# Attention row maxima in one reduce over two PSUM banks, carried to the score row by DMA

## The chip, the cores and the metric

The kernel runs on one core of one Trainium2 chip. The metric is the device time of one execution in microseconds (us). TensorE (PE) multiplies matrices, VectorE (DVE), ScalarE (ACT) and GpSimd (POOL) work on vectors, and every DMA is issued by SyncE (SP), which does nothing else. Each engine takes its instructions in program order, and an instruction that waits holds up everything behind it on its engine.

## The reference, cut to what matters

A two-layer trunk acts on 512 latent tokens of width 1024 with 256 context tokens in front. Each layer has a convolution branch, eight heads of latent attention (MLA) and eight heads of grouped-query attention (GQA), gates that merge the three, an output projection, and a channel mixer (FFN). The attention part, per head:

```python
def attention_block(q, k, v, scale):
    s = jnp.einsum('bqhgd,bkhd->bhgqk', q, k).astype(jnp.float32) * scale
    p = jax.nn.softmax(s, axis=-1)
    return jnp.einsum('bhgqk,bkhd->bqhgd', p.astype(v.dtype), v)
```

Latent queries see all 768 keys. In layer 0 the context queries are computed as well and see the 256 context keys; in layer 1, the last, they are not needed.

## The kernel before

All matrices are split into a high and a low part, and each product is three matmuls. The order of the work is written out by hand: the program is a list of stages, and the order of the code is the order on each engine. Stages of a layer are: norm, convolution branch, latents and token projections, 24 steps of gate projection, `kvproj` (keys and values), attention (`Attention.run`), merge, output projection and FFN. In layer 0, gate steps and FFN steps also call `bg_step`, which streams two 512 KB blocks of modulation weights (`w_mod`) and multiplies them for later use; `mod` holds one PSUM bank open while such a group is under way.

Attention runs 16 heads, 8 GQA then 8 MLA, each in units: in layer 1 six units (six tiles of 128 keys against the 512 latent queries), in layer 0 a seventh one for the context queries. A unit `i` of head `h` does the following, on PE in this order:

- `score(h, i)`: the transposed scores `st` of 128 keys, two passes for GQA, three for MLA. The last pass has one more row of contraction: a row of ones in the keys against a row of the negated row maxima in the queries (`mrow`: row 64 of `q2` in GQA, row 96 of `qh` in MLA). So the maximum is subtracted inside the matmul. ACT then takes exp twice (`pe`, and rounded `ph`), and POOL or DVE the difference `pl`.
- `pv`: three matmuls `ox` of the unit that stands `LAG` = 4 units back. After the last key tile of a head, which therefore falls in unit 3 of the next head (layer 1) or unit 2 (layer 0, whose context part follows in unit 3), DVE copies the sum to `u`. `norm1` then starts the division by the row sums: `sd<-u` writes one row to DRAM, `rc<-sd` reads it back over 128 partitions. Later `norm2` takes the reciprocal, writes it (`sd<-rc`) and broadcasts it (`rb<-sd`). The last two heads of layer 1's order and of layer 0's (`fast`) do it with matmuls, `nt` and `nb`.
- `max_rows(i)` of the **next** head, for `i` below 4: scores of 128 queries against all 768 keys in two matmuls, into two PSUM tiles of one bank (512 and 256 wide), and a maximum by DVE over each. After the fourth, `mcat` takes the larger of each pair into a column set of `mxs`. In layer 0 `max_rows(4)` and `(5)` do the same for the context queries of the head itself.
- transposes for the head after next (`trans_a`, `trans_b`).

In the head's last unit, ahead of the next head's first score, `fin(True)` transposes `mxs` on PE into PSUM (`mt`), and ACT copies four pieces of 1x128, times -1, to the score row. `fin(False)` does two pieces for the context queries in unit 3. For the first head, `kvproj` runs all four `max_rows` one after the other at its third step, and `fin(True)` at its sixth.

PSUM is one pool of 8 tiles of one bank each. In heads 13 to 15 the attention also reloads 16 tiles `rel` from DRAM for the merge (384 KB each in layer 0, 256 KB in layer 1).

Of the kernel before, what the change touches and what calls it, by code (L numbers as in the profile page):

```python
# [47 lines left out]
class Feeder:  # L48
    """Streams weight blocks: DRAM -> raw -> (hi, lo) split, ahead of their use."""

# [45 lines left out]
def trunk_kernel(ctx: ExitStack, tc: tile.TileContext, x_t, ctx_t, cc, vec, grow, ident, rope,  # L96
# [14 lines left out]
    smp = ctx.enter_context(tc.tile_pool(name="smp", bufs=12))  # L111
    psp = ctx.enter_context(tc.tile_pool(name="psp", bufs=8, space=bass.MemoryType.PSUM))
    drp = ctx.enter_context(tc.tile_pool(name="drp", bufs=1, space=bass.MemoryType.DRAM))
    ctx.enter_context(tc.manual_schedule())

    def big(s, dt=F32):
# [8 lines left out]
    def psum(s):  # L125
        return psp.tile([128, 512], F32, tag="ps", name=nm(s))

# [11 lines left out]
    def cpV(o, i):  # L139
        V.tensor_copy(out=o, in_=i)  # L140
# [20 lines left out]
    am = [[const.tile([128, KD, 2], F32, name=f"am{l}{i}") for i in range(2)] for l in range(L)]  # L161
    mxs = [const.tile([128, 128], F32, name=f"mxs{i}") for i in range(2)]
    kr = const.tile([128, 6, ROPE], F32, name="kr")
# [6 lines left out]
    ones_d = dram("ones", [1, T])  # L170
    s_d = [[dram("sd", [2, T]) for _ in range(16)] for _ in range(L)]

    steps = []
# [259 lines left out]
    def setup():  # L433
# [12 lines left out]
        V.memset(cs[:], 0.0)  # L446
        for m in mxs:
            P.memset(m[:], 0.0)
        st["n1"] = Norm(0, 0, st["X"], [XS, CS])
# [12 lines left out]
    def layer(l):  # L462
# [422 lines left out]
        for i in range(24):  # L885
            gate(i)
            if i < 22:
                bg_step()

        def attn_pre(_):  # L890
            st.pop("H"), st.pop("ln")
            gate_spill()
        add([], attn_pre)

# [94 lines left out]
        class Head:  # L989
            def max_rows(self, t):  # L990
                w, k = self.maxq(t)
                if t in (0, 4):
                    self.m2 = small("mx2")
                for i, (c0, n) in enumerate(((0, 512), (512, 256)) if t < 4 else ((512, 256),)):
                    p = psum("mx")
                    mm(p[:, 0:n], lhsT=w, rhs=k[:, c0:c0 + n], start=True, stop=True)  # L996
                    o = 2 * (t % 4) + i
                    V.tensor_reduce(out=self.m2[:, o:o + 1], in_=p[:, 0:n], axis=AX.X, op=ALU.max)  # L998
                if t == 3:
                    self.mcat(True)  # L1000
                if t == 5:
                    self.mcat(False)

            def mcat(self, x):
                mx = mxs[0 if x else 1]
                n = 4 if x else 2
                mv = mx.rearrange("p (a b) -> p a b", b=32)[:, 0:n, 0]
                m3 = self.m2[:, 0:2 * n].rearrange("p (a b) -> p a b", b=2)
                if x:
                    tt(V, mv, m3[:, :, 0], m3[:, :, 1], ALU.max)  # L1010
                else:
                    cpV(mv, m3[:, :, 0])

            def fin(self, x):
                mx = mxs[0 if x else 1]
                p = psum("mt")
                nc.tensor.transpose(p[:, 0:128], mx[:], idn[:])
                for i in range(4 if x else 2):
                    c0 = (0 if x else 512) + i * 128
                    cpA(self.mrow(slice(c0, c0 + 128)), p[32 * i:32 * i + 1, 0:128], -1.0)  # L1020

# [97 lines left out]
        class Attention:  # L1119
# [8 lines left out]
            def prologue(self, i):  # L1128
                hd = self.heads[0]
                if i == 0:  # L1130
                    warm(AF.Exp)
                    hd.trans_a()
                    hd.trans_b()
                elif i == 2:
                    for t in range(4):
                        hd.max_rows(t)
                    self.heads[1].trans_a()
                    self.heads[1].trans_b()
                elif i == 5:
                    hd.fin(True)  # L1140

# [119 lines left out]
            def run(self, _):  # L1261
# [3 lines left out]
                for g in range(len(seq) + LAG):  # L1265
                    h, i = seq[g] if g < len(seq) else (16, g - len(seq))
                    hd = self.heads[h] if h < 16 else None
                    nx = self.heads[h + 1] if h + 1 < 16 else None
                    if nx and i == nu - 1:
                        nx.fin(True)  # L1270
                    if hd:
# [12 lines left out]
                    if hd and not last:  # L1284
                        if i == 0:
                            hd.max_rows(4)
                        if i == 1:
                            hd.max_rows(5)
                        if i == 3:
                            hd.fin(False)  # L1290
                    if hd:
# [33 lines left out]
                st.pop("VT"), st.pop("rl")  # L1325
                self.heads = None
        add([], lambda b: st["A"].run(b))

# [178 lines left out]
        def up(j):  # L1507
# [19 lines left out]
            elif j > 1:  # L1527
# [7 lines left out]
                one(1)  # L1535
                bg_step()

        j0 = done = 0
        for gi, gn in enumerate(GROUPS):
# [24 lines left out]
            j0 += gn  # L1564

    setup()
    bg += [(0, r, kt) for r in (1, 2) for kt in range(KD)]
# [5 lines left out]
    for s in steps:  # L1573
        b = feeder.take(len(s.blocks))
        pump(*s.budget)
        s.fn(b)
        while feeder.n_done < feeder.n_take:
            feeder.release()


# [85 lines left out]
```

## Time and profile before

| | |
|---|---|
| Median of 3 runs | 2548.25 us (2548.14 to 2550.47) |
| Profiled execution, first to last instruction | 2548.6 us (the only time that was recorded of it) |
| TensorE busy | 2395.1 us, 94% |
| VectorE busy | 1612.0 us, 63% |
| ScalarE busy | 1052.0 us, 41% |
| GpSimd busy | 675.9 us, 27% |
| Mean granted TensorE clock | 0.976 |

The profiled execution lies 0.35 us above the median. Layer 0's attention runs from about 535 to 757 us, layer 1's from about 1874 to 2058 us. Busy shares are means over the whole; what an instruction is worth has to be read in the stage where it stands.

### The profile page before, as it was taken

What the parts mean: (1) busy time and instruction counts of PE and PEld (TensorE: products, weight loads), DVE (VectorE), ACT (ScalarE), POOL (GpSimd) and SP (SyncE); (2) the same over time, 40 slices, a digit from 0 to 9 for tenths busy, and PEclk for the clock granted to TensorE, in tenths of its full rate; (3) what the DMA queues carried; (4) which work ended last, traced back from release to release, by engine and by line L of the source; (5) the groups of instructions that cost most, each with busy time, mean ns of one, the idle gap of its engine ahead of it and who ended that gap; (6) DMA issues with size and microseconds to landing.
All of it is one profiled execution on the core that took longest, in us unless ns stands there. A gap on an engine that the chain in (4) does not pass through costs nothing.

```text
span 2548.6 us, 33199 instructions
## 1 busy us (share of the span) xinstructions
PE 2395.1 (94%) x12538; PEld 1954.5 (77%) x12538; DVE 1612.0 (63%) x2669; ACT 1052.0 (41%) x1832; POOL 675.9 (27%) x505
## 2 busy tenths in 40 slices
PE   7977999988999999999999999888989999999999
PEld 4876777766778878888888887776766778888887
DVE  6889773389864465434344458889579865655454
ACT  3453422477751234323232234444376732434332
POOL 1575400136543221000000003433036541201000
PEclk9988999999999999999999999999999999999999
DMA  6111366611144412323322222233421154232332
GB/s 253 56 54 54 118 217 199 230 44 51 42 141 134 162 50 83 103 89 107 99 100 91 92 94 89 66 91 94 148 89 45 29 178 162 75 108 86 101 103 75
DMA packets 109197, 267.71 MB, mean 105 GB/s; under 512 B 20022, under 2 KB 28860, under 8 KB 109036
## 3 DMA queue, kind: packets, MB, share of 16 engines
q1 hardware_dynamic: 109036, 265.58, 31.8%
q8 instruction: 99, 1.62, 0.3%
q14 instruction: 62, 0.51, 0.1%
HBM read 231.31 MB, written 31.60 MB: 103 GB/s over the span
## 4 chain that ended last, share of the span: by engine, by line
PE 59%; DVE 22%; issue 10%; ACT 5%; DMA 2%; POOL 1%; SPq 0%; ACTq 0%; POOLq 0%; DVEq 0%
PE up L223 22%; PE pz L223 16%; PE bx L223 7%; DVE acc L146 6%; DVE lo L143 3%; PE gt L223 2%; DVE mx L998 2%; PE st L1148 2%; PE gl L223 2%; ACT hi L137 1%; PE qp L706 1%; DVE qm L146 1%; DVE rst L143 1%; PE mx L996 1%; PE ox L1177 1%
## 5 line engine op out<-in xcount | busy, mean ns | idle before, releaser
L143 DVE TENSOR_TENSOR lo<-raw,hi 128x1024 fp32r<-128x1024 f32 (+4 forms) x282 | 353.7, 1261 | 475.3 <-ACT hi L137 470.0
L137 ACT ACTIVATE hi<-raw 128x1024 fp32r<-128x1024 f32 (+4 forms) x298 | 283.2, 962 | 422.2 <-PE pz L223 170.9
L223 PE MATMUL up<-hl,hi 128*128 128x512 f32 (+1 forms) x1088 | 333.7, 354 | 6.1 <-DVE hl L146 5.8
L223 PE MATMUL up<-hh,hi 128*128 128x512 f32 (+1 forms) x1088 | 332.6, 353 | 2.0 <-DVE fc L146 2.0
L223 PE MATMUL up<-hh,lo 128*128 128x512 f32 (+1 forms) x1088 | 330.7, 352 | 0.8 <-DVE lo L143 0.8
L143 POOL TENSOR_TENSOR acc<-acc,ct 128x497 f32<-128x497 f32 (+14 forms) x180 | 236.3, 1335 | 283.9 <-ACT ct L137 280.7
L143 POOL TENSOR_TENSOR pl<-pe,ph 128x512 fp32r<-128x512 f32 x176 | 233.8, 1343 | 225.4 <-ACT ph L1157 81.1
L146 DVE SCALAR_TENSOR_TENSOR fc<-up,vct,fc 128x511 f32<-128x511 f32 (+1 forms) x264 | 162.1, 656 | 184.4 <-ACT fc L1485 182.6
L143 POOL TENSOR_TENSOR gl<-fc,gh 128x768 fp32r<-128x768 f32 (+1 forms) x44 | 69.3, 1574 | 784.0 <-ACT gh L137 681.5
L223 PEld LDWEIGHTS up<-hh,hi 128*128 128x128 f32 x1088 | 183.5, 190 | 42.7 <-ACT fc L1485 11.7
L223 PEld LDWEIGHTS up<-hl,hi 128*128 128x128 f32 x1088 | 184.4, 190 | 35.1 <-DVE hl L146 6.6
L223 PEld LDWEIGHTS up<-hh,lo 128*128 128x128 f32 x1088 | 185.3, 191 | 30.7 <-DVE lo L143 1.3
L223 PE MATMUL gt<-hh,lo 128*128 128x512 f32 x576 | 176.2, 360 | 15.5 <-DVE lo L143 15.5
L146 DVE SCALAR_TENSOR_TENSOR acc<-y,vct,acc 128x497 f32<-128x497 f32 (+14 forms) x180 | 185.1, 1074 | 1.6
L223 PE MATMUL gt<-hh,hi 128*128 128x512 f32 x576 | 178.4, 364 | 0.5 <-ACT hi L137 0.5
L223 PE MATMUL gt<-hl,hi 128*128 128x512 f32 x576 | 175.8, 359 | 0.0
L1485 ACT ACTIVATE fc<-up,vct 128x512 f32<-128x512 f32 (+1 forms) x132 | 88.4, 703 | 197.9 <-PE up L223 197.9
L223 PE MATMUL pz<-gl,hi 128*128 128x512 f32 (+1 forms) x528 | 163.5, 358 | 0.0
L223 PE MATMUL pz<-gh,hi 128*128 128x512 f32 (+1 forms) x528 | 163.0, 356 | 0.0
L223 PE MATMUL pz<-gh,lo 128*128 128x512 f32 (+1 forms) x528 | 162.7, 356 | 0.0
L1155 ACT ACTIVATE pe<-st 128x512 f32<-128x512 f32 x208 | 124.4, 599 | 76.5 <-PE st L1148 59.9
L998 DVE TENSOR_REDUCE mx<-mx 128x1 f32<-128x256 f32 (+1 forms) x288 | 139.3, 531 | 20.5 <-PE mx L996 20.2
(300 smaller groups left out, 4846.7 us busy)
## 6 DMA issues: line engine op xcount, KB each, us to landing
raw<-in_w_up_dram SPq DMA_DIRECT2D x88, 512.0 KB
raw<-in_w_mod_dram SPq DMA_DIRECT2D x80, 512.0 KB
raw<-in_w_gate_dram SPq DMA_DIRECT2D x48, 512.0 KB
raw<-in_w_a_dram SPq DMA_DIRECT2D x26, 512.0 KB
gd<-go SPq DMA_DIRECT2D x48, 256.0 KB
gx<-gd SPq DMA_DIRECT2D x48, 256.0 KB
raw<-in_w_dn_dram SPq DMA_DIRECT2D x32, 384.0 KB
raw<-in_w_dn_dram SPq DMA_DIRECT2D x32, 320.0 KB
```

Of the source, the lines that this page charges most:

```text
L137: act(out=o, in_=i, func=AF.Copy, scale=scale)
L143: e.tensor_tensor(out=o, in0=a, in1=b, op=op)
L146: V.scalar_tensor_tensor(out=o, in0=a, scalar=s, in1=b, op0=op0, op1=op1)
L223: mm(p[:, 0:cn], lhsT=w, rhs=a[:, c0:c0 + cn], start=(k == 0 and j == 0), stop=(k == n - 1 and j == 2))
L706: mm(p[i][:, 0:384], lhsT=a, rhs=w[:, i * 384:(i + 1) * 384], start=(k == 0 and q == 0), stop=(k == 2 and q == 2))
L996: mm(p[:, 0:n], lhsT=w, rhs=k[:, c0:c0 + n], start=True, stop=True)
L998: V.tensor_reduce(out=self.m2[:, o:o + 1], in_=p[:, 0:n], axis=AX.X, op=ALU.max)
L1148: mm(p[:], lhsT=a, rhs=b, start=(i == 0), stop=(i == len(ops) - 1))
L1155: act(out=e[:], in_=p[:], func=AF.Exp, scale=hd.scale)
L1177: mm(o[0:65, :], lhsT=vh, rhs=hi[:], start=(t == 0), stop=False)
L1485: act(out=acc[:, c], in_=p[:, 0:s[1]], func=AF.Identity, scale=vcol(o + 1), bias=vcol(V_FB + j + i * KF))
```

## The change

`max_rows` puts its two matmuls into one tile of two banks, and one DVE reduce over 768 columns gives the negated maximum straight into a column of a small tile `mn`. For context queries it is a single bank (`mc`) and a reduce over 256. `mcat`, `fin`, `mxs` and the transposes `mt` are gone. In their place SP issues two DMAs per set of rows: `md<-mn` writes the columns to DRAM in query order, and a second one reads that row into `mrow`. The write goes element by element: neighbours in DRAM come from different partitions.

PSUM is divided anew: 8 single banks outside attention, and from `attn_pre` to the end of `run` 6 single and one double. Since a modulation group would hold a bank through attention, six of the `bg_step` calls move from gate steps of layer 0 to its FFN steps.

```diff
     def psum(s):
-        return psp.tile([128, 512], F32, tag="ps", name=nm(s))
+        return banks["one"].tile([128, 512], F32, tag="ps", name=nm(s))
+
+    def psum2(s):
+        return banks["two"].tile([128, 1024], F32, tag="pd", name=nm(s))
...
             gate(i)
-            if i < 22:
+            if i < 16:
                 bg_step()
...
             gate_spill()
+            psum_layout(6, 1)
...
-                    self.m2 = small("mx2")
-                for i, (c0, n) in enumerate(((0, 512), (512, 256)) if t < 4 else ((512, 256),)):
-                    p = psum("mx")
-                    mm(p[:, 0:n], lhsT=w, rhs=k[:, c0:c0 + n], start=True, stop=True)
-                    o = 2 * (t % 4) + i
-                    V.tensor_reduce(out=self.m2[:, o:o + 1], in_=p[:, 0:n], axis=AX.X, op=ALU.max)
-                if t == 3:
-                    self.mcat(True)
-                if t == 5:
-                    self.mcat(False)
...
+                    self.mn = mnp.tile([128, 8], F32R, tag="mn", name=nm("mn"))
+                if t < 4:
+                    p, n = psum2("mx"), T
+                    for c0, cn in ((0, 512), (512, 256)):
+                        mm(p[:, c0:c0 + cn], lhsT=w, rhs=k[:, c0:c0 + cn], start=True, stop=True)
                 else:
-                    cpV(mv, m3[:, :, 0])
-
-            def fin(self, x):
-                mx = mxs[0 if x else 1]
-                p = psum("mt")
-                nc.tensor.transpose(p[:, 0:128], mx[:], idn[:])
-                for i in range(4 if x else 2):
-                    c0 = (0 if x else 512) + i * 128
-                    cpA(self.mrow(slice(c0, c0 + 128)), p[32 * i:32 * i + 1, 0:128], -1.0)
+                    p, n = psum("mc"), NCTX
+                    mm(p[:, 0:n], lhsT=w, rhs=k[:, NX:T], start=True, stop=True)
+                V.tensor_reduce(out=self.mn[:, t % 4:t % 4 + 1], in_=p[:, 0:n], axis=AX.X, op=ALU.max, negate=True)
+                if t in (3, 5):
+                    t0, nt = (0, 4) if t == 3 else (4, 2)
+                    c = slice(t0 * 128, (t0 + nt) * 128)
+                    md = m_d[l][self.idx][0:1, c]
+                    dma(md.rearrange("o (t p) -> (o p) t", p=128), f(self.mn[:, 0:nt]))
+                    dma(f(self.mrow(c)), md)
...
-                    if nx and i == nu - 1:
-                        nx.fin(True)
...
-                        if i == 3:
-                            hd.fin(False)
...
-                bg_step()
+                bg_step(2 if j in (4, 8, 12, 16) else 1)
```

Three places show how the instructions move. The first is SP in layer 1 in unit 3 of MLA head 1 (`u` and `sd` belong to head 0, whose sum has just been finished; `kh` is a key tile of head 3; `ogd` and what follows stand in the next head). Before:

```order
L1196 DMA sd_213<-u_17783 1x512
L1198 DMA rc_17893<-sd_213 128x4
L1096 DMA kh_17902<-ones_188 1x768
L1243 DMA ogd_186<-oh_17943 128x512
L1244 DMA ogd_187<-ol_17944 128x512
L1203 DMA sd_213<-rc_17893 128x4
L1205 DMA rb_17990<-sd_213 64x512
```

After, where `mn`, `md` and `qh` belong to head 2, whose first score comes three units later (units 4 and 5 of head 1 lie between):

```order
L1196 DMA sd_211<-u_17453 1x512
L1198 DMA rc_17551<-sd_211 128x4
L1021 DMA md_245<-mn_17492 128x4x1
L1022 DMA qh_17458<-md_245 1x512
L1098 DMA kh_17559<-ones_186 1x768
L1243 DMA ogd_184<-oh_17600 128x512
L1244 DMA ogd_185<-ol_17601 128x512
L1203 DMA sd_211<-rc_17551 128x4
L1205 DMA rb_17639<-sd_211 64x512
```

The two new DMAs stand behind both DMAs of `norm1` and ahead of the key row, and the second new one reads what the first wrote.

The second place is PE in layer 1, from the last transpose of unit 4 of MLA head 1 through its unit 5 to the first score of MLA head 2. Before:

```order
L986 MATMUL tp_17935<-idn,qm_14980 96x128
L1017 MATMUL mt_17949<-idn,mxs_96 128x128
L1148 MATMUL st_17955<-ql_17639,kh_17608 128x512
L1148 MATMUL st_17955<-qh_17638,kl_17609 128x512
L1148 MATMUL st_17955<-qh_17638,kh_17608 128x512
L1177 MATMUL ox_17929<-ph_17846,va_16421 65x512
L1178 MATMUL ox_17929<-ph_17846,va_16421 64x512
L1179 MATMUL ox_17929<-pl_17847,va_16421 65x512
L1148 MATMUL st_17968<-ql_17789,kh_17757 128x512
L1148 MATMUL st_17968<-qh_17788,kl_17758 128x512
L1148 MATMUL st_17968<-qh_17788,kh_17757 128x512
```

After, the same stretch:

```order
L1001 MATMUL tp_17592<-idn,qm_14767 96x128
L1148 MATMUL st_17606<-ql_17322,kh_17291 128x512
L1148 MATMUL st_17606<-qh_17321,kl_17292 128x512
L1148 MATMUL st_17606<-qh_17321,kh_17291 128x512
L1177 MATMUL ox_17586<-ph_17508,va_16215 65x512
L1178 MATMUL ox_17586<-ph_17508,va_16215 64x512
L1179 MATMUL ox_17586<-pl_17509,va_16215 65x512
L1148 MATMUL st_17619<-ql_17459,kh_17427 128x512
L1148 MATMUL st_17619<-qh_17458,kl_17428 128x512
L1148 MATMUL st_17619<-qh_17458,kh_17427 128x512
```

The transpose `mt` is gone from ahead of unit 5, and the very last `st` pass, the first that reads the score row of head 2 (row 96 of its `qh`), stands where it stood.

The third place is DVE in layer 0, units 0 and 1 of MLA head 4 (the reduces into `mx_1508`, and those from `mc`, are the head's context rows). Before:

```order
L998 TENSOR_REDUCE mx_1505_6945<-mx_6946 128x1
L998 TENSOR_REDUCE mx_1505_6945<-mx_6949 128x1
L998 TENSOR_REDUCE mx_1508_6952<-mx_6953 128x1
L140 CAST ph_6939<-pe_6938 128x512
L998 TENSOR_REDUCE mx_1505_6945<-mx_6970 128x1
L998 TENSOR_REDUCE mx_1505_6945<-mx_6973 128x1
L998 TENSOR_REDUCE mx_1508_6952<-mx_6976 128x1
L140 COPY mxs_97<-mx_1508_6952 128x2
L140 COPY u_6860<-ox_6861 65x512
```

After:

```order
L1016 TENSOR_REDUCE mn_6729<-mx_6730 128x1
L1016 TENSOR_REDUCE mn_6734<-mc_6735 128x1
L156 CAST ph_6723<-pe_6722 128x512
L1016 TENSOR_REDUCE mn_6729<-mx_6752 128x1
L1016 TENSOR_REDUCE mn_6734<-mc_6756 128x1
L156 COPY u_6650<-ox_6651 65x512
```

Three reduces per unit become two, and the copy to `mxs` is gone from ahead of the copy of `u`; the four-wide `mxs` operation that stood behind the reduces of unit 3 is gone as well.

## Rows read from the trace of the kernel before

**Rows 1.** The page: busy time of each engine; the chain by line.

```profile
PE 2395.1 (94%) x12538; PEld 1954.5 (77%) x12538; DVE 1612.0 (63%) x2669; ACT 1052.0 (41%) x1832; POOL 675.9 (27%) x505
PE up L223 22%; PE pz L223 16%; PE bx L223 7%; DVE acc L146 6%; DVE lo L143 3%; PE gt L223 2%; DVE mx L998 2%; PE st L1148 2%; PE gl L223 2%; ACT hi L137 1%; PE qp L706 1%; DVE qm L146 1%; DVE rst L143 1%; PE mx L996 1%; PE ox L1177 1%
```

**Rows 2.** Windows, busy us (instructions) by engine, PEclk, DMA share, GB/s.

```profile
455.00:500.00 45.00, 44.26 (x263) 35.07 (x262) 18.86 (x21) 20.76 (x31) 7.37 (x4) 1.00 0.76 261
535.00:600.00 65.00, 55.90 (x272) 37.76 (x272) 59.91 (x124) 48.73 (x110) 44.43 (x40) 0.97 0.15 42
643.00:740.00 97.00, 94.29 (x499) 70.30 (x498) 82.48 (x159) 71.75 (x159) 56.05 (x43) 1.00 0.18 58
860.00:1300.00 440.00, 433.02 (x2470) 366.36 (x2470) 202.16 (x302) 129.32 (x181) 40.42 (x24) 0.99 0.27 93
1951.00:2031.00 80.00, 78.06 (x387) 56.69 (x387) 70.89 (x128) 59.20 (x128) 48.40 (x37) 1.00 0.11 28
```

**Rows 3.** Timeline, a handover in layer 1: start, us, line, operation.

```profile
1984.19 0.69 DVE L140 COPY u<-ox 65x512 f32<-65x512 f32 x1 [0.49 <-PE ox L1179]
...
1984.91 0.23 SPq L1196 DMA_DIRECT2D sd<-u  x1
1986.05 0.33 SPq L1198 DMA_DIRECT2D rc<-sd  x1
1986.43 0.27 SPq L1096 DMA_DIRECT2D kh<-ones  x1
...
1987.66 1.11 ACT L137 ACTIVATE qh<-mt 1x128 fp32r<-1x128 f32 x4
...
1988.82 0.49 PE L1148 MATMUL st<-qh,kh 97*128 97x512 f32 x1
```

**Rows 4.** Waits of TensorE, 1875 to 2060: us in total, times, longest.

```profile
PE mt L1017 <- DVE mxs L143: 5.9, 7, 2.3
```

**Rows 5.** Timeline of SyncE, 1970 to 2001.

```profile
1980.66 0.33 SPq L1203 DMA_DIRECT2D sd<-rc  x1
1982.10 0.45 SPq L1205 DMA_DIRECT2D rb<-sd  x1
```

**Rows 6.** Timeline, end of layer 1's attention.

```profile
2044.03 0.24 SPq L1196 DMA_DIRECT2D sd<-u  x1
2047.96 0.33 SPq L1198 DMA_DIRECT2D rc<-sd  x1
...
2049.55 0.18 DVE L1202 RECIPROCAL rc<-rc 128x4 f32<-128x4 f32 x1 [2.01 <-DMA rc<-sd]
...
2044.85 0.42 PE L1148 MATMUL st<-qh,kh 97*128 97x512 f32 x1
```

**Rows 7.** Timeline, start of layer 0's attention.

```profile
514.65 3.79 DVE L998 TENSOR_REDUCE mx<-mx 128x1 f32<-128x512 f32 x8
...
515.77 1.48 PE L986 MATMUL tp<-idn,gt 128*64 128x128 f32 x6
```

**Rows 8.** Groups of `mxs`: ns min/median/max, first, last start, forms.

```profile
L143 DVE TENSOR_TENSOR mxs<-mx x32: 166/194/1122, 518.5 to 2042.5; 128x4 f32<-128x4 f32 x32
L140 DVE COPY mxs<-mx x16: 169/494/1151, 535.5 to 739.8; 128x2 f32<-128x2 f32 x16
```

**Rows 9.** Timeline, layer 0: three heads and the end.

```profile
608.66 0.24 SPq L1196 DMA_DIRECT2D sd<-u  x1
...
611.88 0.50 PE L1148 MATMUL st<-q,kl 65*128 65x512 f32 x1 [0.33 <-ACT q L137]
...
663.32 0.24 SPq L1196 DMA_DIRECT2D sd<-u  x1
...
668.41 0.40 PE L1148 MATMUL st<-qh,kh 97*128 97x512 f32 x1
...
736.67 0.33 SPq L1198 DMA_DIRECT2D rc<-sd  x1
...
736.59 0.40 PE L1148 MATMUL st<-qh,kh 97*128 97x512 f32 x1
```

More of the change, by code (lines that the diff above doesn't have):

```diff
@@ L111, in trunk_kernel, with psum_layout @@
     smp = ctx.enter_context(tc.tile_pool(name="smp", bufs=12))
-    psp = ctx.enter_context(tc.tile_pool(name="psp", bufs=8, space=bass.MemoryType.PSUM))
+    mnp = ctx.enter_context(tc.tile_pool(name="mnp", bufs=4))
     drp = ctx.enter_context(tc.tile_pool(name="drp", bufs=1, space=bass.MemoryType.DRAM))
     ctx.enter_context(tc.manual_schedule())
+    banks = {"open": []}
+    def psum_layout(single, double):
+        for c in reversed(banks["open"]):
+            c.__exit__(None, None, None)
+        uid[0] += 1
+        banks["open"] = []
+        for key, n, w in (("one", single, 1), ("two", double, 2)):
+            if n:
+                c = tc.tile_pool(name=f"ps{key}{uid[0]}", bufs=n, space=bass.MemoryType.PSUM, reuse_waits="tile")
+                banks[key] = c.__enter__()
+                banks["open"].append(c)
     def big(s, dt=F32):
@@ L161, in trunk_kernel @@
     am = [[const.tile([128, KD, 2], F32, name=f"am{l}{i}") for i in range(2)] for l in range(L)]
-    mxs = [const.tile([128, 128], F32, name=f"mxs{i}") for i in range(2)]
     kr = const.tile([128, 6, ROPE], F32, name="kr")
@@ L171, in trunk_kernel @@
     s_d = [[dram("sd", [2, T]) for _ in range(16)] for _ in range(L)]
+    m_d = [[dram("md", [1, T]) for _ in range(16)] for _ in range(L)]
     steps = []
@@ L446, in setup @@
         V.memset(cs[:], 0.0)
-        for m in mxs:
-            P.memset(m[:], 0.0)
         st["n1"] = Norm(0, 0, st["X"], [XS, CS])
@@ L992, in max_rows @@
                 if t in (0, 4):
-                    self.m2 = small("mx2")
-                for i, (c0, n) in enumerate(((0, 512), (512, 256)) if t < 4 else ((512, 256),)):
-                    p = psum("mx")
-                    mm(p[:, 0:n], lhsT=w, rhs=k[:, c0:c0 + n], start=True, stop=True)
-                    o = 2 * (t % 4) + i
-                    V.tensor_reduce(out=self.m2[:, o:o + 1], in_=p[:, 0:n], axis=AX.X, op=ALU.max)
-                if t == 3:
-                    self.mcat(True)
-                if t == 5:
-                    self.mcat(False)
-            def mcat(self, x):
-                mx = mxs[0 if x else 1]
[L1006 to L1010, printed above, removed]
-                else:
-                    cpV(mv, m3[:, :, 0])
-            def fin(self, x):
-                mx = mxs[0 if x else 1]
-                p = psum("mt")
-                nc.tensor.transpose(p[:, 0:128], mx[:], idn[:])
-                for i in range(4 if x else 2):
-                    c0 = (0 if x else 512) + i * 128
-                    cpA(self.mrow(slice(c0, c0 + 128)), p[32 * i:32 * i + 1, 0:128], -1.0)
+                    self.mn = mnp.tile([128, 8], F32R, tag="mn", name=nm("mn"))
[3 more added lines that the diff above has]
+                        mm(p[:, c0:c0 + cn], lhsT=w, rhs=k[:, c0:c0 + cn], start=True, stop=True)
+                else:
+                    p, n = psum("mc"), NCTX
[7 more added lines that the diff above has]
+                    dma(f(self.mrow(c)), md)
         class GHead(Head):
@@ L1138, in prologue @@
                     self.heads[1].trans_b()
-                elif i == 5:
-                    hd.fin(True)
             def score(self, hd, u):
@@ L1326, in run @@
                 self.heads = None
+                psum_layout(8, 0)
         add([], lambda b: st["A"].run(b))
@@ L1564, in layer @@
             j0 += gn
+    psum_layout(8, 0)
     setup()
@@ L1578, in trunk_kernel @@
             feeder.release()
+    for c in reversed(banks["open"]):
+        c.__exit__(None, None, None)
 def _prep(i):
```

## The prediction

> **What bounds the kernel now.** I read the page first: TensorE is busy for 2395 of 2548.6 us, and the chain that ended last is PE for the most part, with FFN and merge matmuls on top; the reduces `mx` hold 2% of it [rows 1]. So the maxima can matter only inside the two attention stages, and there I read the windows [rows 2]. In layer 0 the GQA heads are bound by DVE (59.91 of 65 us busy, PE 55.90). In the MLA heads of both layers PE is the bound: 94.29 of 97 us in layer 0, 78.06 of 80 in layer 1. Little can be won there, and whatever makes PE wait longer shows in full.
>
> Third, I read one handover in the timeline [rows 3], because the row of maxima is a deadline. DVE copies the finished sum `u` at 1984.19; SP issues `sd<-u` at 1984.91, and `rc<-sd`, which has to see it landed, at 1986.05; the next DMA goes out at 1986.43. Meanwhile ACT copies the four pieces of the next row, 1987.66 to 1988.77, and the `st` pass that reads them starts at 1988.82. That pass stands on PE right behind the end of the copies: already before the change the row is just in time. From `sd<-u` to that pass are 3.91 us.
>
> **The change, part by part.** The new row can't come before this chain: `sd<-u` lands (1986.05 less 1984.91, 1.14 us), `rc<-sd` is issued and the next DMA follows (0.38) [rows 3], the write `md<-mn` lands (M), and the read of the row lands (R). SP takes them in this order, and the maxima are ready earlier, so SP's queue decides, not DVE.
>
> M is not in the trace. The nearest row is `sd<-rc`, a write of 128 short pieces: its reader is issued 1.44 us after it [rows 5]. That is the lower bound, as `md<-mn` writes four times as many pieces, of 4 bytes. The upper bound is a one-row write behind reload traffic, 2044.03 to 2047.96, 3.93 us [rows 6]. I take 1.8, close to the lower end, as SP's queue is quiet in most heads. R lies between 1.14 (`sd<-u`, one row the other way [rows 3]) and 1.59 (`rc<-sd` issued at 2047.96, its reader on DVE at 2049.55 [rows 6]); I take 1.35. The chain is 1.14 + 0.38 + 1.8 + 1.35 = 4.67 us from the issue of `sd<-u`, with ends of 4.10 and 7.04.
>
> The Trainium skill speaks against the change here. Its page "DMA: Bandwidth & Descriptors" says under "Rules for kernel authors" that a last dimension that isn't contiguous becomes one descriptor per element, and under "Anatomy of one DMA" that a DMA has about 2.0 us of fixed cost. By that M + R would be an estimated 4.0 us where I take 3.15, and the sum would come out near 2584; the landings shown here, 1.14 to 1.59 us, are all under its 2.0.
>
> *Layer 1, heads.* The handovers of heads 2 to 14 can be read like the one in [rows 3], 13 in number; from `sd<-u` to the pass they add up to 50.56 us, 3.89 each. With 4.67 the pass comes 0.78 later, and as the next `u` hangs on that pass through PE's order, each delay adds to the next: 13 × 0.78 = 10.1 (2.7 with the low end, 41 with the high). What comes back: `mxs` and its 0.2 us in DVE's order [rows 8] and some overlap of reduces, in the four or five GQA heads where `u` is late on DVE: 2 us. The transpose `mt`, for which PE waited 5.9 us in this layer [rows 4], brings nothing, as PE now waits a little further on, at the pass. ACT loses 1.1 us a head, but it isn't the bound. Net **+8**.
>
> *Layer 1, last head.* Here SP issues five reloads ahead of `sd<-u`, and `rc<-sd` follows 3.93 us later, at 2047.96 [rows 6]. `md<-mn` goes out at about 2048.38, the row is there at 2048.38 + 1.8 + 1.35 = 2051.5. Before, the pass ran at 2044.85 [rows 6]. PE stands for the difference, and everything behind it waits for PE: **+6.7** (6.1 to 9.0).
>
> *Start of each attention.* In `kvproj` four `max_rows` stand one behind the other. Before, the eight reduces ran back to back, 3.79 us from 514.65, while PE had left for the next transposes at 515.77 [rows 7]. With one double tile each pair of matmuls has to wait for the reduce before it. Reduces of 0.95 (3.79 / 4) and pairs of about 0.5 (a pass alone takes 0.49 [rows 3]) alternate: 514.65 + 3 × 1.45 = 519.0, so PE leaves 3.2 later. Twice that is 6.4; part is swallowed in layer 0, whose first heads are bound by DVE. **+5** (0 to 6.4). In the heads the units lie further apart than a reduce lasts, and I cost the single double tile at nothing there; the cover is gone when DVE runs a unit behind.
>
> *Layer 0, GQA heads.* Six handovers, 3.85 us on average (one is 608.66 to 611.88, 3.22 [rows 9]), against 4.67: +4.9. But here DVE is the bound and loses work: the four-wide `mxs` and the context copy, whose medians are 0.19 and 0.49 and that take up to 1.1 beside other work [rows 8], and a little in each reduce; about 1.2 us a head, so `u` is ready earlier by as much: −7. Net **−2** (−6 to +12).
>
> *Layer 0, MLA heads.* A head has one more unit here, so the gap is longer: 663.32 to 668.41 is 5.09 [rows 9], the seven average 5.23. The chain of 4.67 fits in. PE's 2.71 us of idle time in 97 [rows 2] bound the gain: **−2**.
>
> *Layer 0, last head.* As in layer 1, `rc<-sd` comes late, at 736.67, with the pass at 736.59 [rows 9]. The row is there at 737.1 + 3.15 = 740.2, 3.7 later for PE. Part of it lies beside the wait for the divisions, which are late as well: **+2.5**.
>
> *At nothing.* The six modulation steps move from a stretch where PE is busy 44.26 of 45 us to one of 433.02 of 440, and DMA from 0.76 to 0.27 [rows 2]: PE pays the same in both, and the weights have more room. The cover would be gone if blocks came late in the FFN. Six banks instead of eight: the two that are missing are those that `mx` took from each round, so a bank comes round after as many units as before. The SP rows behind the new ones (`kh`, `sd<-rc`) have units to spare.
>
> Sum: 8 + 6.7 + 5 − 2 − 2 + 2.5 = +18.2, against the profile's own 2548.6 us: 2566.8. The median of the runs is 0.35 lower, so I forecast **2566 us**.
>
> **The rivals.**
> - *Slower DMAs.* If the scattered write takes 2.4 and the row 1.6, the chain is 5.5, 0.83 longer. That is 10.8 in layer 1, 5 in layer 0's GQA heads, 1.9 in its MLA heads (5.5 against 5.23), 1.7 in the two last heads: **2585**. For it: 512 pieces of 4 bytes, which no row shows. Against it: no quiet small DMA in the rows takes over 1.6.
> - *A wash.* With the low ends (4.10), layer 1's heads cost 0.7, the last heads 6.1 and 1, the starts 3, and layer 0 gives 7.5 back: +3.3, **2552**. For it: 1.44 and 1.14 are measured landings.
> - *Faster.* The place is the handover, and the deciding point is a chain under 3.9 us, the mean gap of layer 1. Then the pass no longer waits for the row, PE keeps the 5.9 us that it spent at `mt` [rows 4], and layer 0 keeps its relief: 3.3 − 5.9 − 4 for starts that stay hidden = −6.6, **2542**. For it: PE, DVE and ACT all have less to do. Against it: four landings in a row would need 3.9 us, and the smallest that the rows show make 4.10.
>
> **How the numbers follow.** The forecast has 0.48 (2554 to 2577), slower DMAs 0.20, the wash 0.17, faster 0.15. A difference under 0.2% (5.1 us) can't be told from none for this kernel. So slower 0.68, same 0.17, faster 0.15. The range reaches into the rivals at both ends, 2541 to 2590, and leaves out about 0.1 on either side.
>
> **What would show it.** Right: in layer 1 PE's waits at `st` name the DMA of the row, about 1 us a head, and some 6 to 7 us in the last head; `md<-mn` to the row's issue is 1.5 to 2.3 us; PE waits for the `mx` reduce at the start of each attention; DVE's window in layer 0 (535 to 600) gets less busy, and the FFN stays as long as it is. Wrong: no wait for the row at all, a write that takes 3 us or more, PE waiting for the double tile in every head, or a time that moves in the FFN or gate stage rather than in attention.

## The result: 18% slower, 2549 to 3002 us

The changed kernel takes 3001.98 us (median of 4 runs, 2999.83 to 3002.52), the kernel before 2549.34 us beside it: a ratio of 1.1768, with a 95% interval of 1.1751 to 1.1785. The forecast was 2566, the range ended at 2590. The direction was right, and the main step of the sum was too small by far.

The page of the changed kernel: busy shares, granted clock in 40 slices, DMA packets, and the chain by engine and by line.

```profile
PE 2491.1 (83%) x12490; PEld 2014.1 (67%) x12490; DVE 1591.4 (53%) x2493; ACT 1011.1 (34%) x1672; POOL 677.4 (23%) x503
...
PEclk9979999767676999999999999999877779999999
...
DMA packets 130539, 267.86 MB, mean 89 GB/s; under 512 B 41318, under 2 KB 50172, under 8 KB 130380
...
PE 59%; DMA 17%; DVE 16%; ACT 4%; issue 3%; SPq 0%; POOL 0%; ACTq 0%; DVEq 0%; POOLq 0%
PE up L239 20%; PE pz L239 13%; DMA md<-mn 12%; PE gt L239 7%; PE bx L239 6%; DVE acc L162 5%; PE st L1148 2%; DVE lo L159 2%; DMA qh<-md 2%; PE mx L1012 2%; DMA sd<-u 1%; PE gl L239 1%; DMA q<-md 1%; DVE mn L1016 1%; ACT hi L153 1%
```

The busy time of PE grew by 96 us, though it has fewer instructions [rows 1], and the chain now holds 17% DMA, 12% of it in the one line `md<-mn`. The granted clock shows two dents, slices 8 to 13 and 29 to 33: the two attention stages. Next, the waits of PE: total us, times, longest.

```profile
PE st L1148 <- DMA qh<-md: 153.5, 16, 13.1
PE st L1148 <- DMA q<-md: 128.6, 14, 11.1
PE st L1153 <- DMA q<-md: 36.4, 8, 9.0
PE st L1153 <- DMA qh<-md: 34.5, 8, 5.5
PE mx L1012 <- DVE mn L1016: 27.6, 18, 3.4
```

Four rows name the new DMA of the score row: 153.5 + 128.6 + 36.4 + 34.5 = 353 us, in nearly every head (L1148 reads the row of the latent queries, L1153 that of layer 0's context queries). The fifth is the double tile. One handover in layer 1 shows the cause, SyncE first (it answers to [rows 3]):

```profile
2410.16 0.22 SPq L1196 DMA_DIRECT2D sd<-u  x1
2411.30 0.34 SPq L1198 DMA_DIRECT2D rc<-sd  x1
2411.73 0.39 SPq L1021 DMA_DIRECT2D md<-mn  x1
2421.37 0.23 SPq L1022 DMA_DIRECT2D qh<-md  x1
```

`sd<-u` lands as before, 1.14 us, and `md<-mn` goes out 0.43 us behind `rc<-sd`, as worked out. But the row can't be issued until 2421.37, **9.64 us** after the write. Over all 48 writes it is 7.22 to 10.29 us, median 8.20. I had taken 1.8. SP's own waits for them, in total, times, longest:

```profile
SPq L1022 <- DMA md<-mn: 382.9, 48, 9.9
```

PE in the same handover:

```profile
2423.13 0.79 PE L1148 MATMUL st<-qh,kh 97*128 97x512 f32 x1 [9.03 <-DMA qh<-md]
...
2426.50 0.63 PE L1148 MATMUL st<-qh,kh 97*128 97x512 f32 x1
...
2431.00 0.39 PE L1148 MATMUL st<-qh,kh 97*128 97x512 f32 x1
```

The first pass with the new row waits 9.03 us, and starts 1.76 us after the row's issue. This handover has a long write and a short read: over the 30 passes that waited for a latent row, issue to pass takes 1.47 to 4.17 us, median 3.36, where I had taken 1.35. Behind the wait the same pass takes 0.63 and later 0.40 us: the granted clock is 0.50 from 2423.0 to 2427.5 (first line below), the lower of PE's two levels, 1.2 in place of 2.4 GHz. The two attention stages in windows follow, which answer to [rows 2]:

```profile
2423.00:2427.50 4.50, 4.37 (x11) 2.98 (x12) 1.38 (x3) 0.88 (x2) 0.18 (x1) 0.50 0.00 0
...
535.00:990.00 455.00, 243.30 (x968) 169.61 (x968) 170.79 (x270) 131.30 (x252) 133.99 (x106) 0.70 0.10 28
2150.00:2480.00 330.00, 190.34 (x721) 128.50 (x719) 150.02 (x214) 112.00 (x209) 103.65 (x87) 0.75 0.11 26
```

PE is busy for 53% and 58% of the stages, with a mean granted clock of 0.70 and 0.75 where the attention windows before had 0.97 to 1.00.

Layer 0 has a second write in each head, for the context row. SP in one of its MLA heads, and DVE's copy of the context part of `u`, the last thing that `sd<-u` needs:

```profile
768.43 0.38 SPq L1021 DMA_DIRECT2D md<-mn  x1
776.30 0.23 SPq L1022 DMA_DIRECT2D qh<-md  x1
776.63 0.24 SPq L1196 DMA_DIRECT2D sd<-u  x1
```

```profile
771.12 0.41 DVE L156 COPY u<-oc 65x256 f32<-65x256 f32 x1
```

`u` is complete at 771.53, but `sd<-u` goes out at 776.63, 5.1 us later, because SP stands at the context row. With it the next head's latent row is late as well. In the kernel before, SP waited for `u` at all 14 `sd<-u` of layer 0; here at none.

To see which stage each experiment moves, the table cuts each profiled execution at starts of PE groups: the first `pk` (`kvproj`), the first `bx` (merge), the first `up` (FFN), the last `gt` (gate of layer 1), the last `pk`, the last `st`. Times in us.

| profiled run | to `pk` | layer 0 attention | merge, project | FFN to gate of layer 1 | `kvproj`, layer 1 | attention, layer 1 | rest |
|---|---|---|---|---|---|---|---|
| before | 506.0 | 251.5 | 177.7 | 915.9 | 21.1 | 180.8 | 495.6 |
| after | 497.8 | 504.2 | 177.9 | 943.0 | 27.2 | 353.0 | 494.9 |
| mod_steps_only | 498.0 | 253.9 | 176.3 | 945.4 | 21.1 | 181.0 | 494.4 |
| reduce_only | 497.1 | 260.2 | 177.9 | 942.6 | 27.6 | 191.7 | 495.6 |
| pieces_16B | 499.4 | 301.9 | 177.9 | 941.8 | 27.4 | 232.9 | 494.3 |
| direct_16B | 497.7 | 258.2 | 176.2 | 942.2 | 27.6 | 198.5 | 494.9 |
| direct_on_before | 508.9 | 250.0 | 177.7 | 915.5 | 21.0 | 191.3 | 494.4 |
| row_dma_first | 505.6 | 252.3 | 176.3 | 918.3 | 21.0 | 184.3 | 496.0 |
| two_doubles | 501.0 | 281.1 | 176.4 | 945.1 | 23.9 | 187.0 | 494.3 |
| spread_steps | 500.4 | 252.4 | 177.7 | 922.4 | 27.1 | 182.4 | 495.1 |

Of the 449.4 us between the two profiled executions, 252.7 lie in layer 0's attention (with its `kvproj`) and 172.2 in layer 1's. But 27.1 came in the FFN, 8.2 went in the gate stage and 6.1 came in `kvproj` of layer 1; reduce_only, which has no such write, shows the same there.

### The profile page after: what moved, and what is told of

Read it like the earlier page. It is cut to its first block, busy times and chain, and to the rows that moved or that the text cites. A ratio compares the mean times of both kernels' runs of the same rounds, so it can differ in the third digit from the quotient of the medians.

```text
span 2998.0 us, 32922 instructions
## 1 busy us (share of the span) xinstructions
PE 2491.1 (83%) x12490; PEld 2014.1 (67%) x12490; DVE 1591.4 (53%) x2493; ACT 1011.1 (34%) x1672; POOL 677.4 (23%) x503
## 2 busy tenths in 40 slices
DMA packets 130539, 267.86 MB, mean 89 GB/s; under 512 B 41318, under 2 KB 50172, under 8 KB 130380
## 4 chain that ended last, share of the span: by engine, by line
PE 59%; DMA 17%; DVE 16%; ACT 4%; issue 3%; SPq 0%; POOL 0%; ACTq 0%; DVEq 0%; POOLq 0%
PE up L239 20%; PE pz L239 13%; DMA md<-mn 12%; PE gt L239 7%; PE bx L239 6%; DVE acc L162 5%; PE st L1148 2%; DVE lo L159 2%; DMA qh<-md 2%; PE mx L1012 2%; DMA sd<-u 1%; PE gl L239 1%; DMA q<-md 1%; DVE mn L1016 1%; ACT hi L153 1%
## 5 line engine op out<-in xcount | busy, mean ns | idle before, releaser
L1016 DVE TENSOR_REDUCE mn<-mx 128x1 fp32r<-128x768 f32 x128 | 121.9, 953 | 372.0 <-PE mx L1012 371.8
L239 PE MATMUL gt<-hh,lo 128*128 128x512 f32 x576 | 176.3, 360 | 14.3 <-DVE lo L159 14.2
L1148 PE MATMUL st<-qh,kh 97*128 97x512 f32 x96 | 47.4, 494 | 153.5 <-DMA qh<-md 153.5
```

The source lines that it names most:

```text
L239: mm(p[:, 0:cn], lhsT=w, rhs=a[:, c0:c0 + cn], start=(k == 0 and j == 0), stop=(k == n - 1 and j == 2))
L1016: V.tensor_reduce(out=self.mn[:, t % 4:t % 4 + 1], in_=p[:, 0:n], axis=AX.X, op=ALU.max, negate=True)
L1148: mm(p[:], lhsT=a, rhs=b, start=(i == 0), stop=(i == len(ops) - 1))
```

## The experiments

The theory after the result: the scattered write is the cause, at 8 us where 1.8 was taken. Its rivals: the single double tile or the division of PSUM; any DMA in this place; and, if it is the write, the number of its pieces rather than where they go.

**reduce_only.** The changed kernel with the row carried as before.

```diff
-                    dma(md.rearrange("o (t p) -> (o p) t", p=128), f(self.mn[:, 0:nt]))
-                    dma(f(self.mrow(c)), md)
...
+                nc.tensor.transpose(p[:, 0:128], mx[:], idn[:])
...
+                    cpA(self.mrow(slice(c0, c0 + 128)), p[32 * i:32 * i + 1, 0:128])
```

> This kernel keeps the two-bank tile, the one negated reduce, the 6 + 1 division of PSUM and the moved modulation steps, and takes the row to its place as before (transpose on PE, copies on ScalarE). Theory: the 450 us lie in the scattered write md<-mn, 7.2 to 10.3 us each time, so without it the time is 2540 to 2556 us: the reduces save a little, the start of each attention costs up to 3.2 us twice. Rival: the division of PSUM or the single double tile makes PE wait; then it stays over 2700 us, with PE waiting for the reduce mx in every head.

Measured: 2592.91 us, ratio 1.0166 (1.0151 to 1.0181). The rival's time falls: over 400 of the 450 us go with the DMAs. But 42 us remain, where I had expected at most 8, and part of them is what the rival named. PE's wait at `mx`, whole run:

```profile
PE mx L1013 <- DVE mxs L1019: 36.3, 26, 3.3
```

And the chain of work at the start of layer 1's attention (start, us, what):

```profile
1888.39 0.88 DVE mxs L1019
1889.31 0.63 PE mx L1013 x2
1889.96 0.97 DVE mxs L1019
1890.97 1.02 PE mx L1013 x2
1892.02 0.97 DVE mxs L1019
```

Reduce, two matmuls, reduce, in strict alternation, 0.9 to 1.0 us for a reduce and 0.6 to 1.0 for a pair: the one double tile is filled and read in turn. `kvproj` gets 6.5 us longer. The heads of layer 1 add 10.9 us (191.7 against 180.8), which I had put at nothing; PE waits 15.1 us at `mx` there, 12 times.

**mod_steps_only.** The kernel before, with the steps moved.

```diff
-            if i < 22:
+            if i < 16:
                 bg_step()
...
-                bg_step()
+                bg_step(2 if j in (4, 8, 12, 16) else 1)
```

> The kernel before, with nothing changed but the six modulation steps moved from gate steps to FFN steps. Theory of the prediction: costs nothing, within 0.2% of before (2543 to 2553). Rival: the weight blocks disturb the FFN, over 2554.

Measured: 2565.18 us, ratio 1.0054 (1.0039 to 1.0068). The rival holds. The gate stage gives 8 us back, the FFN stage takes 29.5 more. Waits of PE in the FFN:

```profile
PE up L223 <- ACT hi L137: 12.5, 3, 4.5
PE pz L223 <- ACT hi L137: 3.8, 1, 3.8
```

At `up` and `pz` of this FFN PE waited 4.8 us in all before and waits 22.7 now, most of it for weights (`hi`) that come late. PE's busy time in the stage grows by 14.9 us, with the moved matmuls and at a granted clock of 0.96 in place of 0.98; what each of the two makes was not separated.

**spread_steps.** Four steps moved, none doubled.

```diff
-            if i < 22:
+            if i < 18:
                 bg_step()
```

> The kernel before with four, not six, modulation steps moved out of the gate stage, so that each FFN step has exactly one and none has two. Theory: in mod_steps_only the FFN lost time because a step with two modulation steps takes four blocks of the weight stream at once and the up weights behind them come late (PE waited 3 to 4.5 us each time); without such steps the time is within 0.2% of before, 2544 to 2554 us. Rival: a step is dearer in the FFN wherever it stands, 2.3 us each; then 2557 or more.

Measured: 2558.82 us, ratio 1.0031 (1.0020 to 1.0043). No wait for `hi` is left in the FFN, and PE's waits at `up` there are 4.8 us again, so the doubled steps did make the weights late. The time is the rival's, though: 8 us remain. But its mechanism isn't in this profile: the FFN stage takes 6.5 us more and the gate stage gives 5.6 back. The profile has 6 of the 8 us in `kvproj` of layer 1, in one wait of 4.4 us for DVE and a stretch at the lower clock (0.82 from 1844 to 1873, where the kernel before has 1.00). Whether each run has that, one profile can't tell; what a step costs outside of the doubled ones stays open.

**pieces_16B.** A query tile takes every fourth query (`mcol(t)` is `slice(t, 512, 4)`, for context queries `slice(512 + t - 4, 768, 2)`), so a partition's four maxima are neighbours in the row.

```diff
-                return self.qs[:, t * 128:(t + 1) * 128], self.kk
+                return self.qs[:, self.mcol(t)], self.kk
...
-                    dma(md.rearrange("o (t p) -> (o p) t", p=128), f(self.mn[:, 0:nt]))
+                    dma(md.rearrange("o (p t) -> (o p) t", p=128), f(self.mn[:, 0:nt]))
```

> Query tile t takes every fourth query (every second of the context queries), so that the four maxima of a partition are neighbours in the row: the write to DRAM goes in 128 pieces of 16 bytes (8 for the context rows) and not in 512 of 4. The row and its values stay the same. Theory: single 4-byte writes are what takes 8 us; the write lands in 1.4 to 1.8 us as sd<-rc does (1.44), and the time is what the prediction worked out for that, 2555 to 2575 us. Rival: any write from 128 partitions in this place takes 8 us (SP's queue, SBUF side), and the time stays near 3000.

Measured: 2677.27 us, ratio 1.0492 (1.0478 to 1.0505). 325 us of the loss are gone, so it is the form of the write, not its place in the queue. Yet it misses the expected band by 100 us; a good part of that is the double tile and the moved steps (42 us in reduce_only). SyncE in a layer 0 MLA head, first a context row in 8-byte pieces, then a row in 16-byte pieces, and PE:

```profile
730.51 0.34 SPq L1024 DMA_DIRECT2D md<-mn  x1
733.63 0.23 SPq L1025 DMA_DIRECT2D qh<-md  x1
734.02 0.24 SPq L1199 DMA_DIRECT2D sd<-u  x1
736.54 0.34 SPq L1201 DMA_DIRECT2D rc<-sd  x1
736.98 0.38 SPq L1024 DMA_DIRECT2D md<-mn  x1
738.44 0.24 SPq L1025 DMA_DIRECT2D qh<-md  x1
```

```profile
741.10 0.50 PE L1151 MATMUL st<-qh,kh 97*128 97x512 f32 x1 [1.95 <-DMA qh<-md]
```

The 16-byte write is read after 1.46 us, as the lower bound had it (median of the 32 latent rows 1.50); the 8-byte ones take about 3 (median of the 16 context rows 3.16). But the pass starts 2.66 us after the issue of the row, where I took 1.35 (median of the 28 that waited 2.50), and `sd<-u` lands after 2.52 and not 1.14. The chain is 2.52 + 0.44 + 1.46 + 2.66 = 7.08 us and doesn't fit even in layer 0's MLA heads, where I had left it 5.23 us. PE waits for the latent row 28 times, 70.8 us in all, and the granted clock is 0.83 to 0.90 in attention windows.

**slots_64B and slots_16B.** 512 pieces of 4 bytes again, each in a slot of its own (`[T, 4]` in place of `[T, 16]` makes slots of 16 bytes).

```diff
-    m_d = [[dram("md", [1, T]) for _ in range(16)] for _ in range(L)]
+    m_d = [[dram("md", [T, 16]) for _ in range(16)] for _ in range(L)]
...
-                    md = m_d[l][self.idx][0:1, c]
-                    dma(md.rearrange("o (t p) -> (o p) t", p=128), f(self.mn[:, 0:nt]))
-                    dma(f(self.mrow(c)), md)
+                    md = m_d[l][self.idx][c, 0:1]
+                    dma(md.rearrange("(t p) o -> p (t o)", p=128), f(self.mn[:, 0:nt]))
+                    dma(f(self.mrow(c)), md.rearrange("c o -> o c"))
```

> As the change, 512 pieces of 4 bytes, but every element has a slot of 64 bytes in DRAM to itself (the row is then read in 512 pieces of 4 bytes, which may be slow of itself and is read apart in the trace). If the 8 us come from neighbours that share a stretch of DRAM, md<-mn lands in 1.5 to 3 us; if a 4-byte write is slow wherever it goes, it still takes over 6 us.

> slots_64B with slots of 16 bytes: 512 pieces of 4 bytes again, four of them in each 64 bytes of DRAM (sixteen in the change, one in slots_64B). It grades the finding that neighbours are what takes the time. If the time grows with the number of pieces that share 64 bytes, md<-mn lands in 2.5 to 4 us, between the 1.88 of slots_64B and the 8.2 of the change; if pieces hold each other up only within 16 bytes, it lands in 1.9 as in slots_64B; if any sharing costs the whole, 7 us or more.

Measured: 2704.72 us for 64 bytes (1.0596, 1.0570 to 1.0623), and 2733.63 us in one run for 16 bytes, with 2547.21 for the kernel before beside it. SyncE in slots_64B, layer 1:

```profile
2139.11 0.38 SPq L1021 DMA_DIRECT2D md<-mn  x1
2140.98 0.52 SPq L1022 DMA_DIRECT2D qh<-md  x1
```

The same 512 pieces of 4 bytes land in 1.87 us here, median 1.88 over all 48 writes. With four in each 64 bytes the median is 2.62, with sixteen 8.20, as the two expectations had it. Number and size of the pieces are the same in the three kernels; only how close they lie differs. The rise isn't even: the latent rows' 512 pieces take 1.90, 2.66 and 8.23 (medians), the context rows' 256 take 1.58, 1.72 and 7.80. Nothing between four and sixteen was tried. The times stay high because PE still waits for the row, 98.7 us for the latent rows in slots_64B, where issue to pass takes 3.57 us (median).

**columns_dram and columns_sbuf.** Each unit sends its own column of 128 maxima as soon as it is reduced, through DRAM or straight to the row.

```diff
+                dma(m_d[l][self.idx][0, t * 128:(t + 1) * 128].rearrange("(p t) -> p t", t=1), f(self.mn[:, t % 4:t % 4 + 1]))
                 if t in (3, 5):
...
+                dma(f(self.mrow(c)).rearrange("o (p t) -> o p t", t=1), f(self.mn[:, t % 4:t % 4 + 1]))
```

(The first line belongs to columns_dram, which keeps the read of the row; the last is the one DMA of columns_sbuf, which drops the other two.)

> As the change, but each unit writes its own column of maxima to DRAM as soon as it is reduced: 128 single pieces of 4 bytes, neighbours in DRAM, instead of 512 pieces at once. Theory: neighbouring 4-byte pieces in DRAM are what takes the time, whatever their number (256 pieces took as long as 512, 7.2 to 10.3 us): the last column still lands after 6 to 9 us and the time stays over 2850. Rival: the number of pieces decides; then a column takes 2 us or less and the time falls to some 2680, as with pieces_16B.

> As columns_dram, but each column goes straight into the score row in SBUF, 128 pieces of 4 bytes, one DMA and no DRAM. Theory that the 8 us belong to 4-byte writes into DRAM: it lands in 1.3 to 2 us, PE hardly waits for it, and the time is that of direct_16B, 2590 to 2610 us. Rival that any single 4-byte pieces are slow: 6 us or more, and a time over 2800.

Measured: 3191.47 us through DRAM (1.2503, 1.2467 to 1.2539), 2600.96 us in SBUF (1.0187, 1.0167 to 1.0207). SyncE in columns_dram, an earlier column with the division's write behind it, then the last column and the row:

```profile
2492.50 0.34 SPq L1017 DMA_DIRECT2D md<-mn  x1
2492.92 0.40 SPq L1202 DMA_DIRECT2D sd<-rc  x1
2500.21 0.45 SPq L1204 DMA_DIRECT2D rb<-sd  x1
...
2509.36 0.38 SPq L1017 DMA_DIRECT2D md<-mn  x1
2517.28 0.23 SPq L1021 DMA_DIRECT2D qh<-md  x1
```

A quarter of the pieces takes 7.92 us, so the rival of the number of pieces falls. And the column holds up what stands behind it: `sd<-rc`, in 16-byte pieces, is read only after 7.29 us, where it took 1.44 before [rows 5]. Into SBUF the same 4-byte neighbours are not slow, and the time is in the expected band. The largest wait of PE for the row in columns_sbuf:

```profile
PE st L1144 <- DMA qh<-mn: 10.3, 5, 5.2
```

In all it waits 15.5 us for the row in 9 times, against 525 us in columns_dram.

**direct_16B.** The query order of pieces_16B, and one DMA from `mn` into the row.

```diff
-                    dma(md.rearrange("o (t p) -> (o p) t", p=128), f(self.mn[:, 0:nt]))
-                    dma(f(self.mrow(c)), md)
+                    dma(f(self.mrow(c)).rearrange("o (p t) -> o p t", t=nt), f(self.mn[:, 0:nt]))
```

> As pieces_16B, but one DMA from SBUF to SBUF, 128 pieces of 16 bytes (8 for the context rows) into the row, without DRAM. Theory: the chain from sd<-u shortens to 1.14 + 0.42 + one landing of 1.3 to 1.6, about 3.1 us, under the mean gap of 3.89 us before, so the row is not waited for and the time is 2530 to 2552 us. Rival: 128 pieces written into one partition come one after the other and land only after 5 us or more: then over 2575 us.

Measured: 2598.28 us, ratio 1.0188 (1.0175 to 1.0201). That is the rival's time, but not its mechanism. Waits of PE:

```profile
PE mx L1015 <- DVE mn L1019: 32.8, 26, 3.2
...
PE st L1149 <- DMA qh<-mn: 7.4, 2, 4.6
...
PE st L1149 <- DMA q<-mn: 4.9, 5, 1.2
```

The latent row is waited for 7 times, 12.3 us, 4.6 of them in one handover; the wait for the double tile is larger, and the moved steps are in here too. By the medians it is 5 us slower than reduce_only, which carries the row by PE and ScalarE, but the runs of the two overlap (2597.08 to 2603.22 against 2589.82 to 2599.82).

**two_doubles.** reduce_only with `psum_layout(4, 2)` in place of `(6, 1)`.

> reduce_only with PSUM divided into 4 single tiles and 2 double ones in attention. Theory: the 36 us for which PE waits at mx for the reduce in reduce_only come from the single double tile; with two they fall under 12 us and the time to 2565 to 2580 us (what is left is the modulation steps). Rival: DVE is late anyway and PE waits as long, or four singles are too few and PE waits at st or tp instead: 2590 or more.

Measured: 2614.83 us, ratio 1.0240 (1.0222 to 1.0258). The rival holds, by its second half. Waits of PE in layer 0's attention:

```profile
PE st L1160 <- DVE qs L159: 13.1, 5, 4.4
...
PE tp L1004 <- DVE kl L159: 4.6, 5, 1.2
...
PE mx L1013 <- DVE mxs L1019: 3.5, 4, 1.9
```

The wait at `mx` falls from 15.8 to 3.5 us there, but with four singles `st` and `tp` wait in turn. Against reduce_only layer 1's two stages gain 8.4 us, layer 0's attention loses 21.

**direct_on_before and row_dma_first.** Could the DMA route win without the rest? The kernel before, with 8 single banks, two reduces and its modulation steps, and one SBUF-to-SBUF DMA for the row; then the same with the DMAs of `norm1` behind the row.

```diff
+                        tt(V, self.mn[:, 0:4], m3[:, :, 0], m3[:, :, 1], ALU.min)
...
+                    dma(f(self.mrow(c)).rearrange("o (p t) -> o p t", t=nt), f(self.mn[:, 0:nt]))
...
-                    if nx and i == nu - 1:
-                        nx.fin(True)
...
+                    if late:
+                        self.norm1(seq[g - LAG][0])
```

(The last two lines are row_dma_first alone.)

> The kernel before, with its 8 single banks, its two reduces per key range and its modulation steps; only the way of the row is new: VectorE takes the smaller of two negated maxima into a tile, query tiles are strided by four as in pieces_16B, and one DMA from SBUF to SBUF in 128 pieces of 16 bytes (8 for the context rows) fills the score row. No PE transposes, no ScalarE copies. Theory: the row is in time in all heads but layer 1's last, the double tile and the moved steps cost nothing here, and PE gets back the 0.1 to 0.3 us of each transpose and part of its waits: 2538 to 2553 us. Rival: SyncE's queue makes the row late in many heads, 2556 or more.

> direct_on_before with one change in order: the two DMAs of norm1 are issued behind the row of maxima, not ahead of it. Theory: SyncE no longer waits for the landing of sd<-u before it issues the row, so the last head of layer 1 loses its 4 to 5 us of waiting: 3 to 6 us under direct_on_before. Rival: the divisions come late by as much, and the time is the same within 2 us.

Measured: 2562.99 us (1.0050, 1.0036 to 1.0063) and 2557.41 us (1.0026, 1.0016 to 1.0037). So the second expectation holds in its size, 5.6 us by the medians, and the first is missed: its rival came, a row that is late in many heads. Waits of PE in layer 1's attention of direct_on_before:

```profile
PE st L1133 <- DMA q<-mn: 11.3, 6, 2.4
PE st L1133 <- DMA qh<-mn: 6.1, 2, 5.6
```

And one handover of row_dma_first, SyncE and PE:

```profile
1935.89 0.51 SPq L1007 DMA_DIRECT2D q<-mn  x1
1936.44 0.44 SPq L1179 DMA_DIRECT2D sd<-u  x1
```

```profile
1937.92 0.47 PE L1133 MATMUL st<-q,kl 65*128 65x512 f32 x1 [1.50 <-DMA q<-mn]
```

From the issue to the pass are 2.03 us, and the issue comes only when the last reduce is done. In layer 1's last head PE's wait falls from 5.6 to 3.1 us, so about half of the 5.6 us gained is shown there and the rest isn't located. No version here beats the kernel before: none of the DMAs that were tried brings the row sooner than PE's transpose and ScalarE's copies.

## Why the prediction was wrong, step by step

- **What bounds the kernel** held: in the MLA heads and at the handover any longer wait of PE showed in full. The row did hang on SyncE's queue, and PE's waits name its DMA. But two of the signs listed as "wrong" came as well: a write of over 3 us, and a time that moved in the FFN and gate stages (27.1 up, 8.2 down).
- **The step that failed** is the price M of the scattered write: "the nearest row is `sd<-rc` ... I take 1.8, close to the lower end". It measured 8.2 (median). The row was near in shape, 128 pieces, but its pieces are of 16 and 24 bytes; what costs is single 4-byte pieces beside one another in DRAM. With slots of 64 bytes the write takes 1.88. Even the upper end, 3.93, was not a bound: it was a write of one whole row behind other traffic, another reason for lateness. From after to pieces_16B the total falls by 325 us.
- **The other DMA times** were taken from the quietest rows. R was 1.35; by the medians it is 3.36 in the changed kernel and 2.50 in pieces_16B. `sd<-u` was 1.14; in layer 0 of the changed kernel its median is 3.04. So the chain of 4.67 isn't reached even with a good write, and layer 0's MLA heads, where it should have fitted in, wait in every head.
- **A term left out.** The sum counts what DVE is spared at the context rows of layer 0, but not their two DMAs. PE waits 70.9 us for these rows (16 times), and their write stands on SP ahead of `sd<-u`: 5.1 us in the head shown above.
- **The clock is not in the sum.** I added waits as they are. After the changed kernel's long waits the passes take 0.63 instead of 0.40 us, and the granted clock of pieces_16B's attention windows is down as well, with waits of up to 5.7 us; so a late handover costs more than its wait. In the two attention stages PE's busy time grew from 393.4 to 480.4 us, with no more matmuls than before: that is the clock's part, some 87 of the 424.9 us lost there. The rest is idle time.
- **The starts**: the alternation was right, and 3.2 us a layer was its price at full clock. Measured are 6.1 to 6.5 us in layer 1: the pairs take up to 1.02 us there and not 0.5, at a granted clock of 0.62 (reduce_only, 1889.3 to 1894.0).
- **"At nothing"**: two costs that were put there are not nothing. The moved steps cost 0.54%, in good part by the way that was named (blocks late in the FFN). The division with the single double tile cost 10.9 us in layer 1's heads; reduce_only less mod_steps_only puts the whole of the tile, starts and banks at some 28 us of the medians. What six banks cost without a double tile was not tried; with four singles and two doubles layer 0's attention loses 21 us more.
- **The last head of layer 1** at +6.7 is borne out in kind: with a quick route (direct_on_before) PE waits 5.6 us in that head, and putting the row ahead of `norm1` brings that to 3.1.
- **The rivals**: slower DMAs was the right one, at M of 2.4 far too small. The faster one needed a chain under 3.9 us. direct_16B keeps to that in most heads, as PE waits for the latent row only 7 times, and still isn't faster, but it carries the double tile and the moved steps; direct_on_before and row_dma_first carry neither, but PE still waits for the row in GQA heads there (11.3 and 10.2 us in layer 1). So what the relief of DVE, ScalarE and PE is worth by itself was not shown.
- **The Trainium skill**, page "DMA: Bandwidth & Descriptors", "Rules for kernel authors", has one descriptor per element in such a write, and the trace agrees: packets under 512 bytes rise from 20,022 to 41,318, and 48 writes hold 32 x 512 + 16 x 256 = 20,480 elements. Its price doesn't lie in that number, as slots_64B has as many. Under "Specifications" the same page of the Trainium skill says that under 512 bytes the DMA engine reads, modifies and writes. That could make neighbours wait for one another, but no run shows the mechanism itself, and 16-byte pieces side by side, which are under 512 bytes too, took 1.50 us. The fixed cost of about 2.0 us, which the prediction took from "Anatomy of one DMA", stands there for DMAs that GpSimd issues; SyncE issues all of these. And not all landings in the rows were under 2.0, as the prediction has it: [rows 6] has 3.93.

## What to carry to other kernels

Before a row moves by DMA, look at the bytes that each piece writes and at what else is written beside them: 4-byte pieces side by side in DRAM took 8 us here, alone in 64 bytes 1.9, and four together as one piece 1.5. Look also at what stands behind the DMA on its queue. A price for an unseen operation is only bounded by a row that has the same feature, not by one of the same size; where no row has it, the range has to be open at the top. And what is costed at nothing should be tried by itself when the change is made: here two such parts cost 1.7% without the DMA.

## What the runs showed of the hardware

- A DRAM write of single 4-byte pieces that are neighbours lands after 7.2 to 10.3 us, whether 256 or 512; a column of 128 took 7.9 in the handover shown. In 8-byte pieces it is about 3 (median 3.16), in 16-byte pieces 1.50 (median).
- What SyncE issues behind such a write lands late too: `sd<-rc` after 7.29 us in columns_dram, 1.44 in the kernel before.
- 128 pieces of 4 or 16 bytes from 128 partitions into one row of SBUF are not slow in this way: the reader starts 2.03 us after the issue in the handover shown. Behind five reloads, in layer 1's last head of row_dma_first, it was 4.55.
- After waits of 9 us PE came back at 1.2 GHz, with passes of 0.63 in place of 0.40 us. After the wait of 1.95 us shown at 741.10 the next passes took 0.40, but those from 742.98 to 745.11 took 0.60 to 0.63 as well, and the granted clock from 741 to 744 was 0.69.
